# Modulation sums finished a quarter later, constants of the convolution loaded first, and the bias rows stored in three pieces

## The chip, the cores and the metric

The kernel runs on 1 core of one Trainium2 chip. The metric is the device time of one execution in microseconds (us). Before the change three runs took 3175.70, 3193.27 and 3194.81 us (median 3193.27); the execution that the profiler recorded took 3181.62 us.

## The reference, cut to what matters

One layer of a streaming trunk, on 2048 prompt tokens and 8 x 16 sample tokens, all in float32. What the change touches is the start (the modulation and the first normed tiles), the constants of the convolution, and the relative bias of the attention.

```python
def trunk_layer(x, c, conv_left, s0, band_cache, w_mod, b_mod, ..., conv_w, ..., rel_bias, w_out, w_up, w_down):
    sh1, sc1, g1, sh2, sc2, g2 = modulation(c, w_mod, b_mod)   # split(silu(c) @ w_mod + b_mod, 6)
    h = rmsnorm(x, norm1_g) * (1 + sc1) + sh1
    proj = h @ w_in
    o_a, conv_state, s = mixer_a(proj, conv_left, s0, conv_w, ...)   # conv of width 4, gated delta rule
    ...
    o_b = band_attention_prompt(qb, kb, vb, rel_bias)                # scores + bias on clipped distance
    x = x + g1 * (jnp.concatenate([o_a, o_b], axis=-1) @ w_out)
    h = rmsnorm(x, norm2_g) * (1 + sc2) + sh2
    x = x + g2 * (jnp.square(jax.nn.relu(h @ w_up)) @ w_down)

def rel_bias_matrix(rel_bias, qpos, kpos):
    d = jnp.clip(qpos[:, None] - kpos[None, :], -(CHUNK - 1), REL_MAX) + (CHUNK - 1)
    return rel_bias.astype(jnp.float32)[:, d]
```

## The kernel before

Tokens go in tiles of 128 rows: 16 prompt tiles and one sample tile (SMP). Phase 1 runs over six blocks of two or three tiles (the first block is tiles 0, 1 and SMP) and makes the projection with `w_in`, the convolution, the delta rule and the first attention; phase 2 runs over five blocks with `w_out`, `w_up` and `w_down`. Each matrix product is made of three matmuls on a high and a low part (`mm3`, L162 to L164, and L519 to L521 in the projection): the input's parts lie in `hT`, the weight's in `w`. `weights` (L166 on) loads a piece of some 0.5 MB into one of three `raw` buffers, ScalarE casts it to the high part (L175), GpSimd subtracts for the low part, and in the first block the low part is stored for later blocks (L184).

Before the first projection stands `modulation_start`: 16 pieces of `w_mod` (0.5 MB each, two halves `u` for each of four quarters `q` of scale and shift) are loaded through `mod_load` (L282), multiplied (`mps`, L288), added to `rows`, and `mod_finish` turns each finished quarter by a matmul (`ptm`, L317) into the columns of `modT`. In it stand also the loads of the three `x` tiles of block one (L261) and, at the end, the constants of the convolution (`conv_consts`: `cwt`, then transposes `psc` on TensorE, L455 and L456). Then `load_hT` norms each tile, transposes it (`psh`, L346), scales it with `modT` (`htmp`) and splits it into `hT`.

`rel_bias` (L1093 on) is called once, at the head of block two. It loads the 8 rows of the bias table (`ext`), makes 8 reversed and padded rows of 768 elements with two DVE copies (L1099, L1100), stores them to `s_ext` in DRAM (L1101), and reads them back shifted, DRAM to DRAM, as `s_bias` (8 x 128 x 640, L1102) and `s_bs` (L1103). The attention reads `s_bias` and `s_bs` from the end of phase 1 on.

The order in which each engine's instructions stand is not that of the code: the tile framework's scheduler places them by its own estimate of time, and each engine then executes its list strictly in that order. All DMAs of the text are issued from one queue, SyncE's (SP); an instruction in it that waits holds up all behind it. PSUM tiles of tag `g` (`mps`, `psg`, `psq`) share three buffers.

Of the kernel before, what the change touches and what calls it, by code (L numbers as in the profile page):

```python
# [19 lines left out]
SMP = 16  # L20
NB = 8
SL = 16
# [16 lines left out]
NPRE = 9  # L39
# [12 lines left out]
class Trunk:  # L52
# [168 lines left out]
    def modulation_start(self, first, tiles, p0):  # L221
# [8 lines left out]
        load = lambda n: self.mod_load(*first[n], p0.tile([P, D], F32, tag="raw0", name="raw0", bufs=NPRE))  # L230
        rvs, xs = [], []
        for n in range(min(NPRE, len(first))):
            rvs.append(load(n))
# [21 lines left out]
        order = list(dict.fromkeys(c[0] for c in first))  # L255
        for n, (sec, q, u) in enumerate(first):
            if n + NPRE < len(first):
                rvs.append(load(n + NPRE))
            if n % 4 == 3 and len(xs) < len(tiles):
                x = self.hp.tile([P, D], F32, tag="x", name="x", bufs=self.nx)  # L260
                nc.sync.dma_start(x, self.x_src(tiles[len(xs)]))  # L261
                xs.append(x)
# [69 lines left out]
    def load_hT(self, tiles, xs, sh, sc):  # L332

        for j, t in enumerate(tiles):
            xn = self.normed(xs[j] if xs else None, t)
            self.load_b(j, self.load_a(t, xn, sh, sc))
            self.fill_step()

    def load_a(self, t, xn, sh, sc):
        nc = self.nc  # L340
        tmps = []
        for q in range(2):
            ks = slice(4 * q, 4 * q + 4)
            ps = self.pa.tile([P, 512], F32, tag=self.patag, name="psh").rearrange("p (k t) -> p k t", t=P)
            for k in range(4):
                nc.tensor.transpose(ps[:, k], xn[:, (4 * q + k) * P:(4 * q + k + 1) * P], self.ident)  # L346
            tmp = self.hp.tile([P, 4, P], F32, tag="htmp", name="htmp", bufs=2)
            tmps.append(tmp)
            if t == SMP:
                f = lambda a: a.rearrange("p k (b s) -> p k b s", s=SL)  # L350
                self.tt(f(tmp), f(ps), bcast(self.modT[:, sc, ks, 1:], 3, SL), ALU.mult)
                self.tt(f(tmp), f(tmp), bcast(self.modT[:, sh, ks, 1:], 3, SL), ALU.add)
            else:
                for k in range(4):
                    a, b = self.modT[:, sc, 4 * q + k, 0:1], self.modT[:, sh, 4 * q + k, 0:1]
                    if k % 2:
                        self.act(tmp[:, k], ps[:, k], AF.Identity, scale=a, bias=b)
                    else:
                        self.ts(tmp[:, k], ps[:, k], a, ALU.mult, b, ALU.add)
        return tmps  # L360

    def load_b(self, j, tmps):
        cs = slice(j * P, (j + 1) * P)
        for q, tmp in enumerate(tmps):
            ks = slice(4 * q, 4 * q + 4)
            self.split(self.hT[:, ks, 0, cs], self.hT[:, ks, 1, cs], tmp)
# [73 lines left out]
    def conv_consts(self, p0):  # L440
        nc, c, i = self.nc, self.p1, self.i
# [5 lines left out]
        for g in range(3):  # L447
            gs = slice(g * 512, (g + 1) * 512)
            t = p0.tile([24, D], F32, tag="cwt", name="cwt", bufs=3)
            w4, h24 = t[0:4, 0:512], t[0:24, 512:1024]  # L450
            nc.sync.dma_start(w4, i["conv_w"][0][:, gs])
            nc.sync.dma_start(h24, i["state_conv"][0].rearrange("b w c -> (b w) c")[:, gs])
            ps = self.pa.tile([P, 512], F32, tag="pa", name="psc")
            for k in range(4):
                nc.tensor.transpose(ps[:, k * 4:(k + 1) * 4], w4[:, k * P:(k + 1) * P], self.ident[0:4, 0:4])  # L455
                nc.tensor.transpose(ps[:, 64 + k * 24:64 + (k + 1) * 24], h24[:, k * P:(k + 1) * P], self.ident[0:24, 0:24])  # L456
            self.ts(self.cw[:, 4 * g:4 * g + 4], ps[:, 0:16].rearrange("p (k r) -> p k r", r=4), 0.5, ALU.mult)
            nc.vector.tensor_copy(self.hists[:, 4 * g:4 * g + 4], ps[:, 64:160].rearrange("p (k r) -> p k r", r=24))
# [569 lines left out]
    def phase1(self):  # L1028
        nc, tc = self.nc, self.tc
        with ExitStack() as st:  # L1030
# [12 lines left out]
            with tc.tile_pool(name="p0", bufs=1, side="right") as p0:  # L1043
                xs = self.modulation_start([(sec, q, u) for q in range(4) for sec in (1, 0) for u in range(2)],
                                           BLOCKS1[0], p0)
# [11 lines left out]
            self.load_hT(B[0], xs, 0, 1)  # L1057
# [34 lines left out]
    def rel_bias(self):  # L1092

        nc = self.nc
        x = self.hp.tile([P, D], F32, tag="big", name="ext", bufs=2)
        ext, rev = x[0:BH, 0:REL], x[32:32 + BH, 0:EXT]
        nc.sync.dma_start(ext, self.i["rel_bias"][0])
        nc.vector.memset(rev[:, EXT - 64:], 0.0)
        nc.vector.tensor_copy(rev[:, EXT - 64 - REL:EXT - 64], ext[:, ::-1])  # L1099
        nc.vector.tensor_copy(rev[:, 0:EXT - 64 - REL], bcast(ext[:, REL - 1], 1, EXT - 64 - REL))  # L1100
        nc.sync.dma_start(self.s_ext, rev)  # L1101
        nc.sync.dma_start(self.s_bias, dram_ap(self.s_ext, P, [[EXT, BH], [-1, P], [1, 640]]))  # L1102
        nc.sync.dma_start(self.s_bs, dram_ap(self.s_ext, P, [[EXT, BH], [-1, SL], [1, 528]]))  # L1103
# [497 lines left out]
```

## Time and profile before

| | us |
|---|---|
| runs, lowest / median / highest | 3175.70 / 3193.27 / 3194.81 |
| profiled execution | 3181.62 |
| its span in the trace | 3179.9 |
| TensorE (PE) busy | 3046.9 |
| VectorE (DVE) busy | 1764.0 |
| ScalarE (ACT) busy | 1472.8 |
| GpSimd (POOL) busy | 644.5 |

All times in the rows are those of the one profiled execution, in us from the start of its span. "Busy" is the time in which an engine has an instruction in hand; PEclk is the clock that TensorE was granted, as a share of full speed. In a list of instructions a bracket gives the time that the engine sat idle before one and what released it.

### The profile page before, as it was taken

How to read it: one execution, taken by the hardware profiler on the slowest of the kernel's cores; microseconds unless marked ns; L12 is line 12 of the kernel's file. 1: busy time of each engine (PE TensorE's matmuls, PEld its weight loads, DVE VectorE, ACT ScalarE, POOL GpSimd, SP SyncE). 2: the span in 40 equal slices, each digit the busy share in tenths (PEclk: the TensorE clock that was granted, in tenths of full speed). 3: DMA queues.
4: the chain of work that ended last, by engine and by line, in shares of the span. 5: the costliest groups of instructions: out<-in, count | busy, mean ns of one | idle time of the engine just before them, and what ended most of it. 6: DMA issues, size and time to landing. Idle time of an engine off the chain costs nothing.

```text
span 3179.9 us, 52984 instructions
## 1 busy us (share of the span) xinstructions
PE 3046.9 (96%) x19649; PEld 2701.7 (85%) x19649; DVE 1764.0 (55%) x4222; ACT 1472.8 (46%) x2803; POOL 644.5 (20%) x517
## 2 busy tenths in 40 slices
PE   6999999999889989999999999999999999999998
PEld 4998989899889878888999888888988877888887
DVE  4775677667878663674356752454745433442223
ACT  3654545555466555545455353444354333333222
POOL 3631211121342247653222200000000000000000
PEclk9999999999999989999999999999999999999999
DMA  8798897888788778876777765666666676856654
GB/s 289 239 294 268 258 284 228 253 250 248 234 268 264 214 229 277 254 250 231 253 238 244 238 214 181 197 193 204 232 198 200 214 236 219 273 173 194 193 190 139
DMA packets 625947, 735.88 MB, mean 231 GB/s; under 512 B 59328, under 2 KB 483248, under 8 KB 623640
## 3 DMA queue, kind: packets, MB, share of 16 engines
q1 hardware_dynamic: 619928, 701.03, 70.1%
q0 software_dynamic: 5760, 31.46, 3.0%
q8 instruction: 155, 2.54, 0.3%
q14 instruction: 104, 0.85, 0.1%
HBM read 619.74 MB, written 115.52 MB: 231 GB/s over the span
## 4 chain that ended last, share of the span: by engine, by line
PE 70%; DMA 13%; DVE 9%; issue 3%; ACT 3%; POOL 1%; SPq 1%; POOLq 0%; ACTq 0%; DVEq 0%
PE psu L1483 7%; PE psu L1482 7%; PE psu L1484 7%; PE psd L164 7%; PE psd L162 7%; PE psd L163 7%; PE psb L163 2%; DMA raw<-in_w_up_dram 2%; PE psb L162 2%; PE psb L164 2%; PE pv L1286 2%; PE psS L1268 2%; PE psq L519 1%; PE psq L521 1%; PE psq L520 1%
## 5 line engine op out<-in xcount | busy, mean ns | idle before, releaser
L175 ACT CAST w<-raw 128x1024 fp32r<-128x1024 f32 (+1 forms) x528 | 552.1, 1047 | 387.1 <-PE psd L164 214.1
L1482 PE MATMUL psu<-hT,w 128*128 128x512 f32 (+2 forms) x1328 | 470.1, 356 | 1.9 <-ACT hT L104 1.7
L1484 PE MATMUL psu<-hT,w 128*128 128x512 f32 (+2 forms) x1328 | 468.5, 354 | 1.4 <-DMA w<-s_w_up 1.4
L1483 PE MATMUL psu<-hT,w 128*128 128x512 f32 (+2 forms) x1328 | 469.2, 354 | 0.4 <-DVE hT L82 0.3
L82 POOL TENSOR_TENSOR w<-raw,w 128x1024 fp32r<-128x1024 f32 (+1 forms) x162 | 391.6, 2427 | 351.3 <-ACT w L175 285.3
L162 PE MATMUL psd<-w,u 128*128 128x512 f32 x1088 | 430.9, 396 | 0.4 <-DVE y L82 0.3
L164 PE MATMUL psd<-w,u 128*128 128x512 f32 x1088 | 429.8, 396 | 0.0
L163 PE MATMUL psd<-w,u 128*128 128x512 f32 x1088 | 426.8, 392 | 2.1 <-POOL w L82 2.1
L79 DVE SCALAR_TENSOR_TENSOR psu<-psu,r 128x512 f32<-128x512 f32 (+2 forms) x160 | 98.9, 618 | 447.0 <-ACT r L92 446.9
L82 DVE TENSOR_TENSOR y<-y,psd 128x512 f32<-128x512 f32 x238 | 162.4, 685 | 260.3 <-PE psd L164 259.3
L1484 PEld LDWEIGHTS psu<-hT,w 128*128 128x128 f32 x1328 | 250.5, 189 | 33.2 <-DMA w<-s_w_up 1.7
L1482 PEld LDWEIGHTS psu<-hT,w 128*128 128x128 f32 x1328 | 250.1, 189 | 33.0 <-ACT hT L104 2.5
L1483 PEld LDWEIGHTS psu<-hT,w 128*128 128x128 f32 x1328 | 250.7, 189 | 31.9 <-issue 1.3
L92 ACT ACTIVATE r<-psu 128x512 f32<-128x512 f32 (+2 forms) x160 | 85.4, 534 | 375.7 <-issue 214.0
L163 PEld LDWEIGHTS psd<-w,u 128*128 128x128 f32 x1088 | 204.6, 188 | 47.8 <-POOL w L82 2.8
L164 PEld LDWEIGHTS psd<-w,u 128*128 128x128 f32 x1088 | 204.2, 188 | 46.4 <-issue 0.4
L162 PEld LDWEIGHTS psd<-w,u 128*128 128x128 f32 x1088 | 204.4, 188 | 43.8 <-DVE y L82 1.0
L162 PE MATMUL psb<-w,hT 128*128 128x256 f32 x816 | 236.0, 290 | 0.9 <-ACT hT L104 0.8
L163 PE MATMUL psb<-w,hT 128*128 128x256 f32 x816 | 234.7, 288 | 0.9 <-DMA w<-s_w_in 0.9
L164 PE MATMUL psb<-w,hT 128*128 128x256 f32 x816 | 233.4, 286 | 1.9 <-DVE hT L82 1.8
L519 PE MATMUL psq<-hT,w 128*128 128x384 f32 (+1 forms) x576 | 196.9, 342 | 8.1 <-ACT ba L499 8.1
L521 PE MATMUL psq<-hT,w 128*128 128x384 f32 (+1 forms) x576 | 193.6, 336 | 0.2 <-DMA w<-s_w_in 0.2
(315 smaller groups left out, 6459.5 us busy)
## 6 DMA issues: line engine op xcount, KB each, us to landing
raw<-in_w_up_dram SPq DMA_DIRECT2D x160, 512.0 KB
raw<-in_w_down_dram SPq DMA_DIRECT2D x160, 512.0 KB
raw<-in_w_in_dram SPq DMA_DIRECT2D x156, 512.0 KB
w<-s_w_down SPq DMA_DIRECT2D x128, 512.0 KB
w<-s_w_in SPq DMA_DIRECT2D x117, 512.0 KB
w<-s_w_up SPq DMA_DIRECT2D x96, 512.0 KB
raw<-in_w_out_dram SPq DMA_DIRECT2D x40, 512.0 KB
x<-in_x_prompt_dram SPq DMA_DIRECT2D x38, 512.0 KB
```

The source lines that it names most:

```text
L79: (eng or self.nc.vector).scalar_tensor_tensor(out, in0, scalar, in1, op0, op1)
L82: (eng or self.nc.vector).tensor_tensor(out, in0, in1, op)
L92: self.nc.scalar.activation(out, in_, func, **kw)
L162: mm(out, lh, rh, start=first, stop=False)
L163: mm(out, lh, rl, start=False, stop=False)
L164: mm(out, ll, rh, start=False, stop=last)
L175: nc.scalar.copy(w[:, 0, 0:n], r)
L519: mm(pc, wh, hT[:, k, 0, 0:T], start=(k == 0), stop=False)
L521: mm(pc, wl, hT[:, k, 0, 0:T], start=False, stop=(k == KT - 1))
L1482: mm(ps[:, c0:c1], wh, h2[:, k, 0, c0:c1], start=(k == 0), stop=False)
L1483: mm(ps[:, c0:c1], wh, h2[:, k, 1, c0:c1], start=False, stop=False)
L1484: mm(ps[:, c0:c1], wl, h2[:, k, 0, c0:c1], start=False, stop=(k == KT - 1))
```

## The change

1. In `modulation_start` the loads come in another order and from more buffers: the constants of the convolution (`cwt`, now two whole loads instead of six pieces) stand behind the second piece of `w_mod`; 12 pieces of `w_mod` are asked for at once (10 own buffers and two of tag `big`) instead of 9, the three `x` tiles in between, and the last four pieces follow as buffers come free.
2. `mod_finish` of a section is called one section later than its sum, so that the next matmuls stand ahead of it. As soon as scale and shift of two quarters are done, half of each `x` tile (4 of 8 pieces of 128 columns) is transposed, scaled and split; before, whole tiles came after all quarters. `conv_consts` is called in the middle, with 12 transposes of 28 rows instead of 24.
3. `rel_bias` is called three times, at the head of blocks two, three and four, with 3, 3 and 2 heads. Its rows lie in a buffer of tag `htmp` instead of `big`, the long row is written in two pieces: four small DVE instructions a call instead of three in all, and five DMAs a call instead of four in all.

```diff
-NPRE = 9
+NPRE = 10
...
+        def load(n):
+            pool, tag, bufs = (self.hp, "big", 2) if n in (NPRE, NPRE + 1) else (p0, "raw0", NPRE)
+            rvs.append(self.mod_load(*first[n], pool.tile([P, D], F32, tag=tag, name="raw0", bufs=bufs)))
+
+        for n in range(min(NPRE + 2, len(first))):
+            load(n)
+            if n % 4 == 3 and len(xs) < len(tiles):
+                x = self.hp.tile([P, D], F32, tag="x", name="x", bufs=self.nx)
+                nc.sync.dma_start(x, self.x_src(tiles[len(xs)]))
+                xs.append(x)
             if n == 1:
+                cwt = p0.tile([28, 1536], F32, name="cwt")
+                nc.sync.dma_start(cwt[0:24], i["state_conv"][0].rearrange("b w c -> (b w) c"))
+                nc.sync.dma_start(cwt[24:28], i["conv_w"][0])
...
+        xs = [self.normed(x, t) for x, t in zip(xs, tiles)]
+        done = []
+
+        def finish():
+            sec, q, row = done.pop(0)
+            self.mod_finish(sec, q, row, self.gp, "g")
+            if sec == first[-1][0] and q % 2:
+                for j, t in enumerate(tiles):
+                    self.load_bq(j, q // 2, self.load_aq(t, xs[j], 0, 1, q // 2))
...
             self.mod_mm(ps, rvs[n], u, u == 0, u == 1)
+            if n == 7:
+                self.conv_consts(cwt)
+            if n + NPRE + 2 < len(first):
+                load(n + NPRE + 2)
             if u:
                 row = rows[:, order.index(sec), q * 256:(q + 1) * 256]
                 self.tt(row, row, ps, ALU.add)
-                self.mod_finish(sec, q, row, self.gp, "g")
-        self.conv_consts(p0)
-        return xs
+                done.append((sec, q, row))
+                if len(done) > 1:
+                    finish()
+        finish()
...
-                if bi == 1:
-                    self.rel_bias()
+                if 1 <= bi <= 3:
+                    self.rel_bias(3 * bi - 3, min(3 * bi, BH))
...
+    def rel_bias(self, h0, h1):
+        nc = self.nc
+        m, k = h1 - h0, EXT - 64 - REL
+        x = self.hp.tile([P, 4, P], F32, tag="htmp", name="ext", bufs=2).rearrange("p a b -> p (a b)")
+        ext, lo, hi = x[0:m, 0:REL], x[32:32 + m], x[64:64 + m, 0:EXT - 512]
+        rev = ext[:, ::-1]
+        nc.sync.dma_start(ext, self.i["rel_bias"][0][h0:h1])
+        nc.vector.tensor_copy(lo[:, 0:k], bcast(ext[:, REL - 1], 1, k))
+        nc.vector.tensor_copy(lo[:, k:], rev[:, 0:512 - k])
+        nc.vector.tensor_copy(hi[:, 0:EXT - 576], rev[:, 512 - k:])
+        nc.vector.memset(hi[:, EXT - 576:], 0.0)
+        nc.sync.dma_start(self.s_ext[h0:h1, 0:512], lo)
+        nc.sync.dma_start(self.s_ext[h0:h1, 512:], hi)
+        o = h0 * EXT + P
+        nc.sync.dma_start(self.s_bias[h0:h1], dram_ap(self.s_ext, o, [[EXT, m], [-1, P], [1, 640]]))
+        nc.sync.dma_start(self.s_bs[h0:h1], dram_ap(self.s_ext, o, [[EXT, m], [-1, SL], [1, 528]]))
```

The scheduler's lists change with it. The first place is SP's queue at the start, from the last pieces of `w_mod` to the fourth piece of `w_in` (before the change; `ext` is the load of the bias table):

```order
L282 DMA raw_189<-in_w_mod_dram 128x4x256
L435 DMA alog<-in_a_log_dram 128x4
L282 DMA raw_196<-in_w_mod_dram 128x4x256
L436 DMA dtb<-in_dt_bias_dram 128x4
L174 DMA raw<-in_w_in_dram 128x4x264 x2
L174 DMA raw<-in_w_in_dram 128x8x128
L1097 DMA ext<-in_rel_bias_dram 8x320
L282 DMA raw_207<-in_w_mod_dram 128x4x256
L373 DMA x<-in_x_prompt_dram 128x1024
L184 DMA s_w_in<-w 128x1056
L174 DMA raw<-in_w_in_dram 128x8x128
```

The same place now:

```order
L302 DMA raw_210<-in_w_mod_dram 128x4x256
L302 DMA raw_218<-in_w_mod_dram 128x4x256
L302 DMA raw_224<-in_w_mod_dram 128x4x256
L443 DMA gdng<-in_gdn_norm_g_dram 128x1
L446 DMA qkg<-in_qn_g_dram 128x64
L447 DMA qkg<-in_kn_g_dram 128x64
L451 DMA alog<-in_a_log_dram 128x4
L452 DMA dtb<-in_dt_bias_dram 128x4
L174 DMA raw<-in_w_in_dram 128x4x264 x2
L174 DMA raw<-in_w_in_dram 128x8x128
L389 DMA x<-in_x_prompt_dram 128x1024 x2
L184 DMA s_w_in<-w 128x1056
```

All 16 pieces of `w_mod` now stand ahead of the small loads and of `w_in`, and the bias table is not in this stretch. The second place is SP's queue a little later, where the bias rows were stored (before):

```order
L174 DMA raw<-in_w_in_dram 128x8x128
L1102 DMA s_bias<-s_ext 1024x1x640
L1103 DMA s_bs<-s_ext 128x1x528
L297 DMA mrow<-in_b_mod_dram 9x256
L184 DMA s_w_in<-w 128x1024
L174 DMA raw<-in_w_in_dram 128x8x128
L373 DMA x<-in_x_prompt_dram 128x1024
```

and where the first of the three pieces stands now, in block two:

```order
L1115 DMA s_ext<-ext 3x512
L1116 DMA s_ext<-ext 3x256
L512 DMA s_sg<-sgw 128x256
L174 DMA raw<-in_w_in_dram 128x8x128
L179 DMA w<-s_w_in 128x1024
L174 DMA raw<-in_w_in_dram 128x8x128
L179 DMA w<-s_w_in 128x1024
L174 DMA raw<-in_w_in_dram 128x8x128
L1118 DMA s_bias<-s_ext 384x1x640
L1119 DMA s_bs<-s_ext 48x1x528
L678 DMA A<-s_U 32x4x32 x12
```

In the pieces for blocks three and four two rows and one row stand between the stores of `s_ext` and the copy to `s_bias`. The third place is DVE at the end of the modulation (before; `rows` are the sums, `bst` statistics of an `x` tile):

```order
L1099 COPY ext<-ext 8x320
L1100 COPY ext<-ext 8x384
L79 SCALAR_TENSOR_TENSOR modT<-ptm,rowT 128x18
L89 TENSOR_SCALAR htmp<-psh,modT 128x128
L82 TENSOR_TENSOR rows<-rows,mps 128x256
L378 BN_STATS bst<-x 128x6 x2
L82 TENSOR_TENSOR hT_98<-htmp,hT_98 128x4x128
L324 COPY modT<-ptm 128x18
```

and now:

```order
L79 SCALAR_TENSOR_TENSOR modT<-ptm,rowT 128x18
L87 TENSOR_SCALAR alog<-alog 128x4
L82 TENSOR_TENSOR htmp<-psh,modT 128x512
L82 TENSOR_TENSOR htmp<-htmp,modT 128x512
L89 TENSOR_SCALAR htmp<-psh,modT 128x128
L82 TENSOR_TENSOR rows<-rows,mps 128x256
L82 TENSOR_TENSOR hT_98<-htmp,hT_98 128x4x128
L344 COPY modT<-ptm 128x18
```

The two copies of `ext` no longer stand ahead of the last sum and of what turns it into `modT`; much of the scaling of the first half of the tiles stands ahead of it instead.

## Rows read from the trace of the kernel before

**Rows 1.** The page: busy time, DMA share in 40 slices, chain of waits.

```profile
PE 3046.9 (96%) x19649; PEld 2701.7 (85%) x19649; DVE 1764.0 (55%) x4222; ACT 1472.8 (46%) x2803; POOL 644.5 (20%) x517
...
DMA  8798897888788778876777765666666676856654
...
PE 70%; DMA 13%; DVE 9%; issue 3%; ACT 3%; POOL 1%; SPq 1%; POOLq 0%; ACTq 0%; DVEq 0%
```

**Rows 2.** Busy time in stretches of 10 us: PE, PEld, DVE, ACT, POOL, PEclk, DMA share, GB/s.

```profile
40.00:50.00 10.00, 4.24 (x23) 3.36 (x24) 8.81 (x13) 4.04 (x9) 5.88 (x4) 0.58 0.89 279
...
70.00:80.00 10.00, 1.90 (x8) 1.58 (x7) 4.29 (x12) 3.41 (x10) 2.35 (x1) 0.78 0.99 335
```

**Rows 3.** Chain that ended last, 28 to 90 us: start, duration, what.

```profile
33.54 7.19 DMA ext<-in_rel_bias_dram
40.76 2.60 DVE ext L1099
43.36 2.41 DVE ext L1100
...
62.39 13.29 DMA x<-in_x_prompt_dram
```

**Rows 4.** Instructions of PE in order of time, 0 to 90 us: start, duration.

```profile
42.08 1.08 PE L288 MATMUL mps<-raw,cT 128*32 128x256 f32 x8 [2.90 <-DMA raw<-in_w_mod_dram]
...
47.75 0.86 PE L317 MATMUL ptm<-sel,rows 128*128 128x9 f32 x4
48.46 0.57 PE L162 MATMUL psg<-w,hT 128*128 128x264 f32 x1
...
70.25 0.33 PE L521 MATMUL psq<-hT,w 128*128 128x384 f32 x1
78.68 0.69 PE L519 MATMUL psq<-hT,w 128*128 128x384 f32 x1 [8.10 <-ACT ba L499]
...
82.61 0.34 PE L519 MATMUL psq<-hT,w 128*128 128x384 f32 x1
...
84.54 0.34 PE L521 MATMUL psq<-hT,w 128*128 128x384 f32 x1
```

**Rows 5.** Instructions of SP's queue, 0 to 90 us: start, time to issue.

```profile
45.80 0.29 SPq L1101 DMA_DIRECT2D s_ext<-ext  x1
...
50.38 0.84 SPq L1102 DMA_DIRECT2D s_bias<-s_ext  x1
51.28 8.49 SPq L1103 DMA_DIRECT2D s_bs<-s_ext  x1
```

**Rows 6.** DMA from 0 to 45 us in 40 slices, and issues with their sizes.

```profile
GB/s 0 29 125 357 379 260 198 344 349 351 348 349 347 349 349 381 378 363 402 358 381 356 229 352 306 108 61 159 243 189 356 383 364 341 295 325 387 402 349 324
...
raw<-in_w_mod_dram SPq DMA_DIRECT2D x16, 512.0 KB
x<-in_x_prompt_dram SPq DMA_DIRECT2D x3, 512.0 KB
```

**Rows 7.** Instructions of ACT and of POOL in order of time, 0 to 90 us.

```profile
37.23 1.07 ACT L175 CAST w<-raw 128x1056 fp32r<-128x1056 f32 x1 [0.42 <-DMA raw<-in_w_in_dram]
...
38.38 7.19 POOL L82 TENSOR_TENSOR w<-raw,w 128x1056 fp32r<-128x1056 f32 x3 [8.95 <-ACT w L175]
```

**Rows 8.** Size of the copy to s_bias, from the list of DMA issues.

```profile
s_bias<-s_ext SPq DMA_DIRECT2D x1, 2560.0 KB
```

**Rows 9.** Busy time in stretches where the pieces now stand, columns as in rows 2.

```profile
230.00:240.00 10.00, 9.85 (x69) 8.81 (x68) 6.87 (x15) 6.10 (x16) 1.97 (x2) 1.00 0.77 225
...
250.00:260.00 10.00, 8.10 (x50) 7.07 (x48) 2.92 (x6) 5.16 (x11) 0.00 (x0) 0.66 1.02 278
...
400.00:410.00 10.00, 10.00 (x59) 10.00 (x58) 4.66 (x21) 1.62 (x3) 1.92 (x1) 1.00 1.09 324
...
490.00:500.00 10.00, 10.00 (x93) 9.72 (x92) 7.90 (x20) 5.85 (x17) 0.00 (x0) 1.00 0.67 191
```

**Rows 10.** Who waited for whom, PE, 225 to 265 us.

```profile
PE ptT L789 <- DMA A<-s_U: 0.2, 1, 0.2
```

More of the change, by code (lines that the diff above doesn't have):

```diff
@@ L255, in modulation_start @@
         order = list(dict.fromkeys(c[0] for c in first))
-        for n, (sec, q, u) in enumerate(first):
[L257 to L262, printed above, removed]
+        xs = [self.normed(x, t) for x, t in zip(xs, tiles)]
[6 more added lines that the diff above has]
+                    self.load_bq(j, q // 2, self.load_aq(t, xs[j], 0, 1, q // 2))
+        for n, (sec, q, u) in enumerate(first):
             if u == 0:
@@ L330, in x_src, with load_aq @@
         return self.i["x_prompt"][0, t * P:(t + 1) * P, :]
[L332 to L337, printed above, removed]
     def load_a(self, t, xn, sh, sc):
+        return [self.load_aq(t, xn, sh, sc, q) for q in range(2)]
+    def load_aq(self, t, xn, sh, sc, q):
         nc = self.nc
[L341 to L344, printed above, removed]
-            for k in range(4):
[L346 to L360, printed above, removed]
@@ new lines, in load_aq @@
+        ks = slice(4 * q, 4 * q + 4)
+        ps = self.pa.tile([P, 512], F32, tag=self.patag, name="psh").rearrange("p (k t) -> p k t", t=P)
+        for k in range(4):
+            nc.tensor.transpose(ps[:, k], xn[:, (4 * q + k) * P:(4 * q + k + 1) * P], self.ident)
+        tmp = self.hp.tile([P, 4, P], F32, tag="htmp", name="htmp", bufs=2)
+        if t == SMP:
+            f = lambda a: a.rearrange("p k (b s) -> p k b s", s=SL)
+            self.tt(f(tmp), f(ps), bcast(self.modT[:, sc, ks, 1:], 3, SL), ALU.mult)
+            self.tt(f(tmp), f(tmp), bcast(self.modT[:, sh, ks, 1:], 3, SL), ALU.add)
+        else:
+            for k in range(4):
+                a, b = self.modT[:, sc, 4 * q + k, 0:1], self.modT[:, sh, 4 * q + k, 0:1]
+                if k % 2:
+                    self.act(tmp[:, k], ps[:, k], AF.Identity, scale=a, bias=b)
+                else:
+                    self.ts(tmp[:, k], ps[:, k], a, ALU.mult, b, ALU.add)
@@ L362, in load_b, with load_bq @@
+        return tmp
     def load_b(self, j, tmps):
-        cs = slice(j * P, (j + 1) * P)
         for q, tmp in enumerate(tmps):
-            ks = slice(4 * q, 4 * q + 4)
-            self.split(self.hT[:, ks, 0, cs], self.hT[:, ks, 1, cs], tmp)
+            self.load_bq(j, q, tmp)
+    def load_bq(self, j, q, tmp):
+        cs, ks = slice(j * P, (j + 1) * P), slice(4 * q, 4 * q + 4)
+        self.split(self.hT[:, ks, 0, cs], self.hT[:, ks, 1, cs], tmp)
     def normed(self, x, t, st=None):
@@ L438, in phase1_consts, with conv_consts @@
         self.ts(self.alog, self.alog, -1.0, ALU.mult)
-    def conv_consts(self, p0):
-        nc, c, i = self.nc, self.p1, self.i
+    def conv_consts(self, t):
+        nc, c = self.nc, self.p1
         self.cw = c.tile([P, 12, 4], F32, name="cw")
@@ L446, in conv_consts @@
         self.hists = c.tile([P, 12, NB * 3], F32, name="hists")
[L447 to L452, printed above, removed]
-            ps = self.pa.tile([P, 512], F32, tag="pa", name="psc")
[L454 to L458, printed above, removed]
+        for g in range(6):
+            gs = slice(g * 256, (g + 1) * 256)
+            ps = self.pa.tile([P, 512], F32, tag="pa", name="psc")
+            for k in range(2):
+                nc.tensor.transpose(ps[:, k * 28:(k + 1) * 28], t[0:28, gs.start + k * P:gs.start + (k + 1) * P], self.ident[0:28, 0:28])
+            pv = ps[:, 0:56].rearrange("p (k r) -> p k r", r=28)
+            self.ts(self.cw[:, 2 * g:2 * g + 2], pv[:, :, 24:28], 0.5, ALU.mult)
+            nc.vector.tensor_copy(self.hists[:, 2 * g:2 * g + 2], pv[:, :, 0:24])
     def conv(self, y, pre, c, n, sub=None):
@@ L1043, in phase1 @@
             with tc.tile_pool(name="p0", bufs=1, side="right") as p0:
-                xs = self.modulation_start([(sec, q, u) for q in range(4) for sec in (1, 0) for u in range(2)],
-                                           BLOCKS1[0], p0)
+                self.modulation_start([(sec, q, u) for q in range(4) for sec in (1, 0) for u in range(2)],
+                                      BLOCKS1[0], p0)
             self.mod_todo = [(sec, q, u) for sec in (2, 3, 4, 5) for q in range(4) for u in range(2)]
@@ L1056, in phase1 @@
             last = len(B) - 1
-            self.load_hT(B[0], xs, 0, 1)
             for bi, tiles in enumerate(B):
@@ L1089, in phase1 @@
         self.ap2 = self.ctx.enter_context(tc.tile_pool(name="p2att", bufs=1, space=bass.MemoryType.PSUM, side="right"))
-    def rel_bias(self):
+    def rel_bias(self, h0, h1):
         nc = self.nc
[L1095 to L1103, printed above, removed]
+        m, k = h1 - h0, EXT - 64 - REL
[12 more added lines that the diff above has]
+        nc.sync.dma_start(self.s_bs[h0:h1], dram_ap(self.s_ext, o, [[EXT, m], [-1, SL], [1, 528]]))
     def softmax(self, ap, ps, bias, n):
```

3 lines of the change are left out of this document (removed).

## The prediction

> **What bounds the kernel now.** I read the page first: TensorE (PE) is busy for 3046.9 of 3179.9 us and holds 70% of the chain that ended last [rows 1]. So only some 133 us of idle PE time are to be had in all, and an edit pays only where PE stands or runs at a low clock. Next the stretches of 10 us, to find where that is at the start. From 40 to 50 us PE is busy for 4.24 us and is granted 0.58 of its clock, from 70 to 80 us for 1.90 us at 0.78 [rows 2]. The chain between 28 and 90 us names the two causes, and both are the bias table [rows 3]. First, a chain goes from the load of `ext` (33.54, 7.19 us) through the two DVE copies (2.60 and 2.41 us). PE meanwhile finished its last but one piece of `w_mod`, waited 2.90 us for the last one until 42.08, and reached `ptm` only at 47.75 and the projection (`psg`) at 48.46, since the last sum stood behind the copies on DVE [rows 4]. Second, 13.29 us pass from the issue of an `x` tile of block two at 62.39 to its landing [rows 3], and its statistics stand on DVE ahead of the last `sgw`; that `sgw` and `ba` keep the PSUM buffer which the third group of `psq` needs, and PE stands for 8.10 us until 78.68 [rows 4]. The reader is to see on SP's queue why that tile was late: `s_ext` is issued at 45.80, `s_bias` at 50.38, and the issue of `s_bs` takes 8.49 us, until 59.77, with `w` and `x` loads queued behind [rows 5].
>
> **What the earlier and denser loads bring.** All 16 pieces of `w_mod` and three `x` tiles, 19 loads of 512 KB (the sample tile is one of them, of the same size), are 10.0 MB. Full slices of the start move some 350 GB/s [rows 6]. The first three of the 40 slices (3.4 us) bring next to nothing; 10.0 MB at 350 GB/s are 28.5 us, the small constants about 1 us, so the last piece of `w_mod` should land near 33 us instead of 42.08. Before, three pieces of `w_in` and the small loads stood ahead of it, and eight slices (the 23rd to the 30th: 229, 352, 306, 108, 61, 159, 243, 189) fell short of 350 GB/s by what is worth 3.7 us [rows 6]. The `w_in` pieces now come behind, 1.5 us each: the first lands at 34.5 us, or at 38.2 if that short stretch, in which the small loads were issued, comes back. ScalarE's cast takes 1.07 us and GpSimd's subtraction 7.19/3 = 2.40 us [rows 7], so the first low part is ready at 38.0 to 41.7 us and one more follows each 2.4 us. PE can begin with the high part before that, but not run freely. I take an effective start 8 us earlier, about 40.5. Bounds: 4.4 us if the loads gain nothing and only the copies are gone (last `mps` at 42.08 and 1.08 long, so `ptm` near 43.3 instead of 47.75); 12 us if PE starts on the high part at 36.5.
>
> **What the missing stall brings.** The stall is 8.10 us, and after it PE runs slowly: 12 matmuls from 78.68 to 82.61 take 3.93 us, the 11 from 82.61 to 84.54 take 1.93, so 0.175 each, and 1.8 us are lost on the 12 [rows 4]. Together 9.9 us. I count them whole: the third `x` tile of block two is now asked for when its buffer comes free, not behind a standing queue. Bounds: 9.9, or 4 if the statistics of that tile, which still stand ahead of the last `sgw` on DVE, are late again by half.
>
> **What costs nothing.** TensorE's 12 fewer transposes and DVE's six more small constant copies lie in the first 35 us, in which PE waits for DMA anyway: the cover is the landing of `w_mod` at 33 us; without it they would be worth some 2 us. The two `cwt` loads move ahead of 14 pieces and delay them by less than 1 us, which I counted. Halved tiles and the later `mod_finish` move PE, DVE and ACT work under the same cover, and take a wait of PE for the sums off each quarter.
>
> **What the three pieces cost where they stand now.** The data are the same: 2560 KB of `s_bias` [rows 8] read and written, with `s_bs` 5.8 MB, at the 324 GB/s of a crowded stretch 18 us of DMA, which now fall in blocks two to four near 230, 400 and 490 us of the old trace (there stand the neighbours that the new order shows). Those stretches have DMA shares of 0.77, 1.09 and 0.67, and of 1.02 some 20 us behind the first [rows 9]. A piece of three heads needs 6.6 us. The full share is about 1.1, so the first piece finds about 3 us of room within 10 us, the second none, the third 4, and the rest pushes `w` pieces back. Against that stand four `w` buffers, and PE waited for DMA only 0.2 us between 225 and 265 us although DMA was as busy [rows 10]. SP itself also stands: from `s_ext` to `s_bias` 4.6 us passed before [rows 5]; in the second and third call two rows and one row lie between, so nearly all of it is a wait in the queue, and with it 3/8 of the 8.49 us, together up to 7.8 us in which no weight is asked for. One `psq` group is 24 matmuls of 0.175 us, 4.2 us a weight, so three weights in hand cover 12.6 us. Bounds: 0 (all hidden) and 18 (all DMA time exposed). I take 4, nearer to the 0.2 us of rows 10.
>
> On DVE the copies come back as nine in three calls. Before they took 2.60 and 2.41 us for 8 rows [rows 3], while GpSimd's three subtractions ran without a gap from 38.38 to 45.57 [rows 7]; where they go now GpSimd is busy for 1.97, 1.92 and 0.00 us of 10 [rows 9]. By the old durations a call costs DVE 7.5 us, and the same 12.6 us of PSUM and weights in hand cover it, so I count 0. The Trainium skill ("SBUF — State Buffer", section Who interferes with whom) says that a DVE copy in a two-port mode and a GpSimd instruction exclude each other for the whole instruction. The trace agrees so far: the copies end with the subtractions (45.77 and 45.57). By that rule the nine would be short here and the 0 is safe; by the old durations it rests on the cover. Against the split speaks another page ("DMA: Bandwidth & Descriptors", section Two DMAs through the same engine are not ordered): a DMA that reads what another wrote has to wait for its semaphore, so three calls pay three such waits. The trace shows one, the 4.6 us of rows 5; three would be 14 us of standing queue, which is the fourth case below.
>
> **The sum.** 3181.6 - 8 - 9.9 + 4 = 3167.7 us against the profiled execution. That one lies 11.7 us under the median of the runs shown, and 4.7 under the mean of the four times (3186.4). I forecast a median of new runs, so I add 4.7: 3172 us, 0.7% under the old median and 0.4% under the mean. The scheduler also moves rows all through phase 1; for that I count 0, and 6 us either way.
>
> **The rivals.**
> - The start gains, the moved bytes give it back: PE keeps standing for `w` in blocks two and three. For it: DMA share 1.09 near 400 us. Against: rows 10. All 18 us exposed: 3181.6 - 17.9 + 18 = 3182, with the 4.7 us 3186.
> - The change does not do what it says in its second half: `x` is late again and the stall only moves. For it: the order on DVE is the same at that place. Against: what kept SP is gone. 3181.6 - 8 + 4 = 3178, with 4.7 us 3182.
> - Everything comes off: 12 + 9.9 + 2 us and nothing given back: 3158, with 4.7 us 3162.
> - Slower: SP's queue stands in each call for `s_ext` and in `s_bs`, 7.8 us three times, 23 us, and the 18 us of bytes come on top: 3181.6 - 17.9 + 41 = 3205, with 4.7 us 3209. It decides once a standing queue outlasts the 12.6 us of weights in hand, so when DMA is full at the moment of the wait. Near 400 us it is; near 490 it is not.
>
> **How the numbers follow.** Forecast 0.62; bytes give it back 0.13; stall stays 0.09; everything comes off 0.12; slower 0.04. The range goes from 3152 (the best case less 10 us of run-to-run spread; the runs shown spread over 19 us) to 3195 (the first two rivals and the same spread); the slowest case lies outside. A measurement of this kernel can tell about 1% from no change, 32 us. Faster by over 1% is under 3161: most of the best case's lower half and a little of the forecast's, 0.10. Slower by over 1% is over 3225: 0.02. Within 1%: 0.88.
>
> **What would show it.** In the profile after, the last `mps` should begin near 33 us and the first `psg` between 36 and 41; no wait of PE above 3 us between there and 90 us; clock 1.0 from 70 to 80 us; SP's `s_bs` issues of about 3 us each. PE waits for `w` behind the new `s_bias` rows would show the second case, a wait of `psq` for `ba` or `sgw` the third. The prediction is wrong if the first 100 us gain under 8 us, or if PE's idle time between 200 and 550 us grows by over 10.

## The result and the profile after

The changed kernel takes 3222.51 us at the median (4 runs, 3215.62 to 3226.73), the kernel before 3190.07 us in the same comparison: a ratio of 1.0107 with a 95% interval of 1.0069 to 1.0145. It is slower by 32 us, where 3172 and a small gain were forecast, and it lies outside the range. The profiled execution took 3222.25 us, with a span of 3220.5 at a mean granted clock of 0.973.

To see where the time goes, I matched the instructions of PE in the two traces (same line, tiles and shape, n-th with n-th) and took the start after less the start before. The table gives medians over stretches of 50 us, named by their first microsecond in the trace of before; a negative number means that the row's kernel is ahead. The other rows are the experiments below. Each row rests on one execution: the one of before is 8.5 us quicker than that kernel's median (3181.62 against 3190.07), the one of e1_spread16 5 us slower than its own (3182.09 against 3177.09), so the last columns are not the differences of the medians.

```
lag behind before, us      50    150    200    250    350    400    500    550    900   1000   1200   1450   3050
after                    -8.8  -10.5   -9.2   -3.9   -2.3    6.4   16.6   21.6   28.8   36.4   41.0   45.9   40.5
e2_mod_only              -7.3    0.3    4.0   -0.9   -1.8   -4.8    1.9    1.9   -2.5   -0.1    1.0   -1.3   -3.0
e3_split_only            -1.3    1.1   -1.4    5.2    4.6   13.2   32.0   34.7   36.1   37.1   48.9   52.6   52.2
e1_spread16             -10.1  -11.8  -10.0   -8.4   -6.2   -3.1    0.3    1.6   -1.1    3.3    6.4    5.8    0.7
e6_spread4              -10.4  -11.9  -10.1   -1.6    0.9   10.5   13.5   14.8    6.8   13.7   16.2   14.9   14.0
e6_spread2               -9.8  -12.0   -9.5    6.4    8.9   26.8   32.4   36.5   27.6   31.3   33.1   30.7   28.1
e7_pool_queue            -9.0  -10.5   -8.7   -3.1    1.7    7.5   18.5   23.9   27.8   35.8   41.4   42.2   42.2
e9_two_calls             -9.0  -10.4   -8.9   -2.4    0.1    9.4   13.4   13.4   21.7   26.5   27.2   32.9   30.3
e10_split_spread         -1.8   -1.9   -3.8   -2.8   -0.8    2.2    6.0    7.0    6.2   19.1   24.6   29.8   26.5
```

So the start gains some 10 us and keeps it to 200 us. By 550 us another 31 are lost, from -9.2 to +21.6. In medians over 10 us three steps stand out where the three calls of `rel_bias` are: -9.4 to -3.9 near 240, -2.3 to 6.4 near 410 and 16.9 to 21.6 near 530, together 18.9 us. Another 10.5 us (6.4 to 16.9) go between 430 and 520, most of them before the changed kernel issues its third copy at 514.65. A second, slower loss of 24 us follows between 550 and 1450.

**The start.** PE's instructions in order of time (start, duration, what; in brackets its idle time and who ended it). They answer to [rows 4]:

```profile
34.58 1.08 PE L308 MATMUL mps<-raw,cT 128*32 128x256 f32 x8 [0.41 <-DMA raw<-in_w_mod_dram]
...
38.35 1.08 PE L308 MATMUL mps<-raw,cT 128*32 128x256 f32 x8
...
40.44 0.48 PE L162 MATMUL psg<-w,hT 128*128 128x264 f32 x2
...
52.56 0.39 PE L162 MATMUL psg<-w,hT 128*128 128x264 f32 x1 [1.94 <-ACT hT L104]
...
68.12 0.33 PE L533 MATMUL psq<-hT,w 128*128 128x384 f32 x1
73.00 0.55 PE L566 MATMUL ptq<-ident,kq 128*128 128x128 f32 x3 [4.54 <-DVE kq L79]
...
74.08 0.52 PE L531 MATMUL psq<-hT,w 128*128 128x384 f32 x1
74.40 0.52 PE L532 MATMUL psq<-hT,w 128*128 128x384 f32 x1
```

The projection begins at 40.44 us against 48.46, and the stall of 8.10 us for `ba` is gone. In its place PE stands 4.54 us for `kq`, and after it runs matmuls 0.32 us apart, against 0.175 before the stand. The granted clock there is 0.50 (columns as in [rows 2]), the lower of the two levels (1.2 GHz of 2.4):

```profile
75.00:77.00 2.00, 2.00 (x8) 2.00 (x8) 2.00 (x3) 0.39 (x1) 1.87 (x2) 0.50 0.66 224
```

DVE and POOL show what `kq` waited for:

```profile
60.87 2.25 DVE L79 SCALAR_TENSOR_TENSOR u<-x 128x12 f32<-128x12 f32 x1
...
64.69 2.19 DVE L82 TENSOR_TENSOR z<-u,z 128x12 f32<-128x12 f32 x1
...
67.32 2.49 DVE L79 SCALAR_TENSOR_TENSOR u<-u,w2s 128x12 f32<-128x12 f32 x2
...
69.99 0.16 DVE L79 SCALAR_TENSOR_TENSOR u<-u,w2s 128x12 f32<-128x12 f32 x1
...
72.39 0.55 DVE L79 SCALAR_TENSOR_TENSOR kq<-psq,y 128x384 f32<-128x384 f32 x1
```

```profile
60.69 2.40 POOL L82 TENSOR_TENSOR w<-raw,w 128x1024 fp32r<-128x1024 f32 x1 [3.33 <-ACT psq L538]
64.44 2.41 POOL L82 TENSOR_TENSOR w<-raw,w 128x1024 fp32r<-128x1024 f32 x1 [1.34 <-ACT w L175]
67.21 2.37 POOL L82 TENSOR_TENSOR w<-raw,w 128x1024 fp32r<-128x1024 f32 x1 [0.36 <-ACT w L175]
```

Three instructions of twelve elements a row, which elsewhere in this chain take 0.16 us, take over 2 us each; the first two end with the subtraction on GpSimd (63.12 and 63.09; 66.88 and 66.85). Before, GpSimd was busy for 8.28 us between 50 and 75 us, now for 15.88. The order on DVE matters as well: before, `z<-u,z` took 2.04 us beside a subtraction too, but `kq` stood ahead of it there and did not wait:

```profile
80.69 0.56 DVE L79 SCALAR_TENSOR_TENSOR kq<-psq,y 128x384 f32<-128x384 f32 x1
...
81.63 2.04 DVE L82 TENSOR_TENSOR z<-u,z 128x12 f32<-128x12 f32 x1
```

**The three steps.** SP's queue at the first call (start, time to issue), which answers to [rows 5]:

```profile
223.42 1.30 SPq L1118 DMA_DIRECT2D s_bias<-s_ext  x1
224.79 7.41 SPq L1119 DMA_DIRECT2D s_bs<-s_ext  x1
232.24 13.19 SPq L678 DMA_DIRECT2D A<-s_U  x12
```

The DMA from 225 to 250 us in 40 slices of 0.6 us, first the busy share in tenths of the 16 engines and then GB/s:

```profile
DMA  9999993212112113332323222112301212356679
GB/s 346 331 399 338 314 274 107 91 74 82 74 78 82 74 79 102 95 98 83 94 83 99 92 81 82 74 74 81 67 13 19 32 31 47 108 159 84 59 236 347
```

While SP has loads to issue, the DMA falls to some 75 to 105 GB/s and one to three tenths, for about 14 us. The trace's DMA records name the reason. The copy `s_bias<-s_ext` is made of rows of 2560 bytes, 0.103 us each, and they run in as many places at once as the copy has heads: 384 rows in 12.8 us at the first call (3.1 at once on the mean), 384 in 13.1 at the second (3.0), 256 in 13.25 at the third (2.0). Before, 1024 rows took 13.27 us, 7.9 at once. A piece of three heads thus lasts as long as the whole of eight, 128 rows one after the other. The trace of before had it to be read; this is its DMA from 50 to 75 us:

```profile
DMA  8999999997555555555799689955569789999789
GB/s 227 220 220 301 380 426 370 347 342 252 215 205 209 209 205 205 213 201 205 284 397 356 234 290 381 350 208 201 217 229 265 273 344 385 368 395 344 232 245 346
```

Nine slices stand at five tenths and 201 to 215 GB/s: half of the 16 engines' time is used, as with 8 of them at work. The waits of PE in the changed kernel around the three calls (us in total, times, longest), which answer to [rows 10]:

```profile
PE ptT L801 <- DMA A<-s_U: 8.8, 2, 8.5
...
PE psq L533 <- DMA w<-s_w_in: 10.1, 1, 10.1
...
PE kS L832 <- DVE E L82: 5.3, 1, 5.3
```

Each is one long stand, in 215 to 265, 380 to 460 and 490 to 560 us. Before, the longest in these three were 1.8 us, 2.9 us and none:

```profile
PE pw L796 <- ACT TW L92: 1.8, 1, 1.8
...
PE ptq L554 <- DVE kq L79: 2.9, 1, 2.9
```

The third stand is an indirect one. The chain behind `E` begins with a small load that took 8.09 us to land, at DMA shares of 1.02 to 1.07; the third copy had ended at 529.7:

```profile
534.17 8.09 DMA X<-s_vt
```

The stretches of 25 us show that the clock falls with the first two (columns as in [rows 2]):

```profile
225.00:250.00 25.00, 16.20 (x92) 14.23 (x91) 6.31 (x12) 6.16 (x17) 0.00 (x0) 0.80 0.43 127
...
395.00:420.00 25.00, 14.89 (x76) 14.52 (x76) 6.78 (x26) 6.17 (x14) 2.96 (x2) 0.80 0.65 197
```

Before, these stretches had PE busy for 24.85 and 22.08 us at clocks of 1.00 and 0.93, with DMA shares of 0.88 and 1.07:

```profile
225.00:250.00 25.00, 24.85 (x190) 22.05 (x189) 17.26 (x48) 12.36 (x31) 2.04 (x2) 1.00 0.88 247
...
395.00:420.00 25.00, 22.08 (x114) 20.50 (x113) 17.59 (x58) 9.82 (x24) 2.96 (x2) 0.93 1.07 322
```

The loss between the second and the third step is of another kind. PE stands for three short waits (0.6, 2.4 and 1.2 us) and then works for 15 us at a clock of 0.50, with no copy of bias rows under way:

```profile
490.00:505.00 15.00, 14.27 (x116) 11.97 (x117) 7.91 (x20) 8.52 (x19) 0.00 (x0) 0.50 0.65 191
```

### The profile page after: what moved, and what is told of

Its sections match the earlier page's. It is cut to its first block, busy times and chain, and to the rows that moved or that the text cites. A ratio compares the mean times of both kernels' runs of the same rounds, so it can differ in the third digit from the quotient of the medians.

```text
span 3220.5 us, 52996 instructions
## 1 busy us (share of the span) xinstructions
PE 3068.7 (95%) x19637; PEld 2719.4 (84%) x19637; DVE 1782.4 (55%) x4237; ACT 1472.6 (46%) x2803; POOL 646.0 (20%) x517
## 4 chain that ended last, share of the span: by engine, by line
PE 69%; DMA 13%; DVE 9%; ACT 3%; issue 2%; SPq 2%; POOL 2%; ACTq 0%; DVEq 0%; POOLq 0%
PE psu L1498 7%; PE psu L1500 7%; PE psu L1499 7%; PE psd L164 7%; PE psd L162 7%; PE psd L163 7%; DMA raw<-in_w_up_dram 2%; PE pv L1302 2%; PE psq L531 2%; PE psS L1284 2%; PE psq L532 2%; PE psq L533 1%; PE pso L162 1%; PE psb L162 1%; PE psb L163 1%
## 5 line engine op out<-in xcount | busy, mean ns | idle before, releaser
L533 PE MATMUL psq<-hT,w 128*128 128x384 f32 (+1 forms) x576 | 194.0, 337 | 10.1 <-DMA w<-s_w_in 10.1
```

Of the source, the lines that this page charges most:

```text
L533: mm(pc, wl, hT[:, k, 0, 0:T], start=False, stop=(k == KT - 1))
```

## The experiments

The theory (A in the expectations): this copy from DRAM to DRAM is spread over as many DMA engines as its outermost dimension has entries, here heads. Three short copies then hold two or three engines for 13 us each, and every load over all 16 that is queued later ends no sooner than its share on those. The rivals: the bytes themselves and the standing of SP's queue for `s_ext` (B); the new order of the work (C).

**e1_spread16: the changed kernel, each head's copy with an outermost dimension of 16.** The rows of `s_ext` are stored 16 times, so that the outermost dimension steps forward from one stored row to the next while the rows inside still step back.

```
-        nc.sync.dma_start(self.s_bias[h0:h1], dram_ap(self.s_ext, o, [[EXT, m], [-1, P], [1, 640]]))
+        for h in range(m):
+            nc.sync.dma_start(self.s_bias[h0 + h].rearrange("(a b) c -> a b c", a=16),
+                              dram_ap(self.s_ext, o + h * 16 * EXT, [[EXT - 8, 16], [-1, 8], [1, 640]]))
```

> The changed kernel with one thing altered: each row of s_ext is stored 16 times, so that each head's copy to s_bias has an outer dimension of 16 (and s_bs as well), one copy a head. Theory A (a copy runs on as many DMA engines as it has heads, each engine moves 128 rows of 0.103 us, 13 us however few the heads, and the transfers behind it in the queue end no sooner): the copies of a call take 2 to 3 us together instead of 12.8 to 13.3, PE's waits of 8.5 us for A and of 10.1 us for w are gone, and the 25 to 30 us lost near the three calls come back: 1.000 to 1.006 of the kernel before. Theory B (the queue stands for s_ext and the bytes are too many for these blocks): the waits for s_ext and the bytes are the same and there are more issues, so 1.009 to 1.013. Theory C (the new order of phase 1 costs it, wherever the copies are): 1.008 to 1.012, with the losses at the same places.

Measured: 3177.09 against 3187.19 us, 0.9966 [0.9951, 0.9981], faster than both kernels, and better than theory A had it; B and C, which forecast a loss of 0.8 to 1.3%, miss. The three copies take 3.4, 3.9 and 4.2 us (2 to 3 were expected), and the DMA stays nearly full at the second call, where it had fallen to 75 GB/s:

```profile
DMA  8983989998999799999999999999999999999999
```

(395 to 420 us). The step near 240 us shrinks from 5.3 to 1.6 us, that at 400 from 8.7 to 3.1; a wait of 5.7 us for `w` stays there. The order of the work on every engine is again another one than the changed kernel's, so this run alone does not part the copies from the order; the runs with 2 and 4 below do.

**e2_mod_only and e3_split_only: each half of the change alone.** The first leaves `rel_bias` in one call at its old place, the second leaves the start as before.

```
e2:  the diff without   -  if bi == 1: self.rel_bias()   and the new rel_bias
e3:  only               +  if 1 <= bi <= 3: self.rel_bias(3 * bi - 3, min(3 * bi, BH))   and the new rel_bias
```

> Parts 1 and 2 alone: the changed kernel with the bias rows made and stored in one call at the head of block two, as before. Theory A: one copy of 13 us on 8 DMA engines instead of three on 3, 3 and 2, so no loss near 230, 400 and 500 us: 0.994 to 1.000 of the kernel before. Theory B: the same, 0.994 to 1.000. Theory C: the order of phase 1 is new here too, 1.002 to 1.010.

> Part 3 alone: the kernel before with the three calls of 3, 3 and 2 heads. Theories A and B: some 10 us gained at the start, where the copy is gone, and 30 to 45 us lost from the three calls on: 1.005 to 1.012 of the kernel before. Theory C: 0.997 to 1.003.

Measured: the start alone 3183.28 us, 0.9987 [0.9969, 1.0004], no difference that can be told; the split alone 3232.57 us, 1.0151 [1.0119, 1.0183], more than any theory expected. The loss belongs to the split. The start's own gain needs the bias table out of its way: alone it is 7.3 us ahead at 50 us and level at 150. And moving the table away gains nothing alone either (+1.1 at 150): the two gains don't add up from the halves, they come together.

**e4_before_spread16: the kernel before, its one call spread over 16.**

```
-        nc.sync.dma_start(self.s_ext, rev)
+        nc.sync.dma_start(self.s_ext, bcast(rev, 1, 16))
```

and the copy by heads as in e1.

> The kernel before, one call, with each head's copy spread over 16 engines as in e1_spread16. Theory A: the copy that held 8 engines for 13.3 us now takes some 7 us on all 16; a stall of 8 us at 70 to 78 us gets shorter: 0.996 to 1.000 of the kernel before. Theories B and C: no change, 0.998 to 1.002.

Measured: 3187.97 us, 1.0005 [0.9988, 1.0021]. The hoped for gain is not there. The copies still take 13.4 us (61.12 to 74.53), in two bursts of 6.2 and 4.9 us, though the DMA's busy share is now seven to nine tenths meanwhile, not five (50 to 75 us, slices of 0.6 us):

```profile
DMA  4799544679999999778999998999999999999999
```

Other loads share the engines. So at that place the spread bought no time that can be told.

**e6_spread2 and e6_spread4: e1 with 2 or 4 in place of 16.** Every engine runs the same instructions in the same order as in e1; only the shape of the copy differs.

```
-            ... rearrange("(a b) c -> a b c", a=16),  [[EXT - 8, 16], [-1, 8], [1, 640]]
+            ... rearrange("(a b) c -> a b c", a=2),   [[EXT - 64, 2], [-1, 64], [1, 640]]
```

> e1_spread16 with one number altered: each head's copy to s_bias has an outer dimension of 2 instead of 16, so that it runs on 2 DMA engines; every engine's list of instructions is that of e1_spread16, row for row. Theory A (few engines make a copy long, and what is queued behind it ends no sooner): three heads take 3 x 64 rows x 0.103 us = 19.8 us, two heads 13.2, so the loss is at least that of the changed kernel: 1.008 to 1.018 of the kernel before. Theory B (the wait for s_ext, the bytes and the issues cost it): all as in e1_spread16, 0.995 to 0.999. Theory C (the order costs it): the order is that of e1_spread16, 0.995 to 0.999.

> The same with an outer dimension of 4. Theory A: 9.9 us for three heads and 6.6 for two, of which the weights in hand cover a part: between e1_spread16 and e6_spread2, 0.998 to 1.006 of the kernel before. Theories B and C: 0.995 to 0.999.

Measured: 3214.23 us with 2, 1.0078 [1.0053, 1.0102]; 3191.21 with 4, 0.9999 [0.9982, 1.0015]; 3177.09 with 16. Against the runs of before made beside each, that is +25, +2 and -10 us: the same bytes in the same order cost 12 us more on 4 and 35 us more on 2. The steps at the three calls, read as for the changed kernel, are 2.0, 3.1 and 3.1 us with 16 (8 together), 8.9, 9.6 and 3.2 with 4 (22) and 16.2, 17.9 and 9.3 with 2 (43). The copies take 19.2, 19.8 and 13.2 us on 2 and 10.0, 11.1 and 7.2 on 4. Three heads at 64 rows of 0.103 us, two abreast, are 19.8 us one head after the other, and the records show 2.0 rows at once: so the three copies of a call seem to use the same two engines, not two each. The waits for weights near 400 us, in e1, with 4 and with 2:

```profile
PE psq L533 <- DMA w<-s_w_in: 5.7, 1, 5.7
```

```profile
PE psq L533 <- DMA w<-s_w_in: 12.3, 1, 12.3
```

```profile
PE psq L533 <- DMA w<-s_w_in: 20.6, 1, 20.6
```

These runs also bound what the copies explain. With 4 the steps at the calls (22 us) are no smaller than the changed kernel's (18.9), yet that kernel ends level with before. And with 2 the copies are longer than the changed kernel's, yet the ratio is no higher (1.0078 [1.0053, 1.0102] against 1.0107 [1.0069, 1.0145]). So a part of the changed kernel's loss is not in the steps that the copies make.

**e7_pool_queue: the changed kernel with the two copies issued from GpSimd's queue.**

```
-        nc.sync.dma_start(self.s_bias[h0:h1], ...)
+        nc.gpsimd.dma_start(self.s_bias[h0:h1], ...)
```

> The changed kernel with the copies to s_bias and s_bs issued from GpSimd's queue instead of SP's; heads, sizes and calls are as in the changed kernel. Theory A in its first form (later transfers of SP's own queue stand behind the long copy, and SP stands in the issue of s_bs): the other queue lets them pass, 0.996 to 1.003 of the kernel before. Theory A in its second form (the two or three DMA engines themselves are taken for 13 us, whatever the queue): 1.005 to 1.011. GpSimd's own wait for s_ext should cost little, it is busy for under 2 of 10 us there.

Measured: 3222.30 us, 1.0112 [1.0080, 1.0143], as slow as the changed kernel. SP no longer stands in `s_bs`, yet PE's wait for `A<-s_U` is the same 8.8 us in total, now with a longest of 5.8:

```profile
PE ptT L801 <- DMA A<-s_U: 8.8, 2, 5.8
```

SP's queue shows that the stand has only moved to the next loads:

```profile
222.15 1.16 SPq L174 DMA_DIRECT2D raw<-in_w_in_dram  x1
223.36 17.87 SPq L678 DMA_DIRECT2D A<-s_U  x12
```

7.41 + 13.19 = 20.6 us in the changed kernel, 17.87 here. On this queue the first copy is of 192 packets of 5120 bytes, 2.8 at once, 13.4 us: no shorter; the other two take 16.8 and 17.1 us. The other queue gained nothing.

**e9_two_calls: the changed kernel with calls of 4 and 4 heads.**

```
-                if 1 <= bi <= 3:
-                    self.rel_bias(3 * bi - 3, min(3 * bi, BH))
+                if 1 <= bi <= 2:
+                    self.rel_bias(4 * bi - 4, 4 * bi)
```

> The changed kernel with two calls of four heads (blocks two and three) in place of calls of 3, 3 and 2 heads. Theory 'few engines a copy': each piece has 4 heads, so 4 engines for the same 13 us (128 rows of about 0.103 us), two such stretches in place of three: the copies take 12.5 to 14 us each on about 4.0 engines, the lag of the third stretch (+15 us in the changed kernel between 475 and 550) is not there, and the ratio is 1.001 to 1.008, under the 1.011 of three calls. Rival 'by bytes': the same 5.8 MB are moved, so the loss is that of three calls, 1.009 to 1.014, and a piece of 4 heads lasts a third longer than one of 3.

Measured: 3207.41 us, 1.0059 [1.0037, 1.0082]. The copies take 13.2 and 13.3 us at 4.0 at once: a third more bytes in each, no more time. There is no third step (9.4 at 400, 13.4 at 500 and at 550 us); of the 15 us that the changed kernel loses between 400 and 550, only 4.7 were a step at its third call. The ratio is in the theory's range and its interval under the rival's: the rival by bytes falls.

**e5_one_call_spread: e1 with one call of eight heads in block two.**

```
-                if 1 <= bi <= 3:
-                    self.rel_bias(3 * bi - 3, min(3 * bi, BH))
+                if bi == 1:
+                    self.rel_bias(0, BH)
```

> e1_spread16 with one call of 8 heads at the head of block two instead of three calls; eight copies on 16 engines, about 7 us together, where the first of the three pieces stands. Theory A: no worse than e1_spread16, 0.994 to 0.999 of the kernel before; if the bytes in a crowded block cost something after all, 0.998 to 1.002.

Measured: 3193.89 us, 1.0011 [0.9996, 1.0027], slower than e1 by medians, although its profiled execution is ahead of before until 1100 us (-5.3 at 1000) and of e1's from 350 to 1450. That execution loses 11 us between 1000 and 1200, and why, the trace does not tell; it is also 10 us quicker than the median of this kernel (3183.91 against 3193.89), so it cannot show all of the difference. What holds is that one call is not better than three once the copies are spread.

**e10_split_spread: the split alone (e3) with the copies spread as in e1.**

```
 e3, and in rel_bias:
+        for h in range(m):
+            nc.sync.dma_start(self.s_bias[h0 + h].rearrange("(a b) c -> a b c", a=16), ...)
```

> Part 3 alone (three calls in blocks two to four, the start as before), with every row of s_ext stored 16 times and one copy a head with an outer dimension of 16, as in the kernel that beat both. Part 3 alone with 3, 3 and 2 engines stood at 1.0151 [1.0119, 1.0183]. Theory 'few engines a copy': the loss was the engines' number, so it goes: each head's copy takes 3 to 5 us, no lag against before grows by more than 4 us over 225-260, 395-430 or 510-545, and the ratio is 0.997 to 1.004. Rival 'moving the work out of the start costs in itself' (the order of the work in blocks two to four, the DVE's copies, the wait for s_ext): the ratio stays over 1.008 although the copies are short. Both expect 0 to 5 us at the start from fewer bytes there.

Measured: 3210.31 us, 1.0066 [1.0044, 1.0088], between what the two theories expected. Up to 900 us the theory holds: copies of 3.3, 5.3 and 3.6 us, and the lag at 550 us is 7.0 against 34.7. But then 24 us are lost again, between 900 and 1450 us, long after the last copy. That is as much as the changed kernel loses between 550 and 1450, and short copies don't cure it. Against e1, which also has short copies and differs by the start, and with it in the order of all that follows, e10 is 32 us slower by medians (+22 and -10 against before). Three stretches of 50 us with their granted clock, 0.81, 0.91 and 0.80:

```profile
900.00:950.00 50.00, 45.43 (x395) 40.27 (x395) 30.04 (x89) 30.28 (x67) 15.52 (x17) 0.81 0.93 287
...
950.00:1000.00 50.00, 46.63 (x359) 44.32 (x358) 39.95 (x125) 30.14 (x71) 14.41 (x17) 0.91 0.54 170
...
1150.00:1200.00 50.00, 38.17 (x243) 34.30 (x242) 36.38 (x87) 27.21 (x54) 21.70 (x15) 0.80 0.62 199
```

Before, it was 0.90, 1.00 and 0.93 there; in the changed kernel 0.94, 0.79 and 0.77. No one wait of PE accounts for it.

## Why the prediction was wrong, point by point

**The loads at the start: right, but not all of it lasted.** An effective start 8 us earlier, about 40.5, was taken; `psg` began at 40.44, and the lag is -8.4 at 56 us. The last wait for a piece of `w_mod` ended at 34.58, near the 33 that was worked out; the last `mps` itself began at 38.35, behind transposes. From 64 to 70 us, just ahead of the old stall, the lag is -6.3: PE had stood 1.94 us for `hT` until 52.56 and then run some matmuls 0.32 us apart.

**The missing stall: half right, and mis-sized.** The wait for `ba` is gone, and DVE read the `x` tiles without a wait. Of the 9.9 us only about 4 came (-6.3 just ahead of the old stall, -10.4 from 120 us on). The prediction said that the stall goes and asked only whether the same tile would be late; it did not ask what stands next. That was the DVE chain from `ba` to `kq`, 12.3 us (60.66 to 72.94), three links of which sat behind GpSimd's denser subtractions, and on DVE `kq` now stood behind them. The Trainium skill ("SBUF — State Buffer", section Who interferes with whom) says that a DVE instruction with two SBUF inputs contends with a GpSimd instruction that reads SBUF; the trace agrees for `z<-u,z` (2.19 us, with a subtraction over it). The prediction used that section for the copies alone, and there its 0 was right: they took 0.35, 0.21 and 0.25 us.

**The three pieces: wrong, the step that failed.** The prediction priced them by bytes: 5.8 MB at 324 GB/s, 18 us between "all hidden" and "all exposed", and took 4; "a piece of three heads needs 6.6 us". It measured 12.8 to 13.3 us a piece whatever its heads, and steps of 18.9 us at the three calls. The bound of 18 was none, since it assumed that all engines work on the copy: with 2 abreast the same bytes make steps of 43 us. A row's time and the number of copies abreast were both in the trace of before (128 rows of 0.103 us behind each other, half of the engines busy), and cutting 8 heads into 3, 3 and 2 keeps the first and lowers the second. The runs show it by dose: 16, 4 and 2 abreast in one and the same order give -10, +2 and +25 us against before, and calls of 4 and 4 heads last as long as calls of 3.

The Trainium skill ("DMA: Bandwidth & Descriptors", sections Why a DMA increments its semaphore by 16 and not by 1 and Rules for kernel authors) has the rule: the slowest dimension that is not 1 sets how many engines a transfer uses, at most 16, and an outermost dimension of fewer confines it to at most that many. The trace agrees (8 heads 7.9, 4 heads 4.0, 3 heads 3.1, 2 heads 2.0). By it the sum would have held three stretches of 13 us on a few engines in place of 18 us of DMA spread over all. The prediction looked at that page for the wait between two transfers and not for this.

**The new order: put at nothing, and it was not.** "The scheduler also moves rows all through phase 1; for that I count 0, and 6 us either way." In the changed kernel 10.5 us are lost between the second and the third step, with PE at a clock of 0.50 for 15 us and no copy under way, and 24 us after 550. e6_spread4, with the same steps at the calls, has neither in that size (1.2 and 0.1 us), and e10 and e1, both with short copies, end 32 us apart. So something that comes with the new order, the clock included, seems to be worth more than 6 us; that it is the order itself is not shown.

**SP's queue.** The slower rival named the place, `s_bs` standing three times with weights queued behind, and came near (3209, against 3222.5), but at a chance of 0.04 and by another road: it let SP stand for `s_ext` and added the bytes. The stand in `s_bs` was put at 3/8 of 8.49 us, about 3; it was 7.41, 5.92 and 5.25 us, longer than the bytes explain; what it waits for is not shown. As e7 shows, the stand is a symptom: without it the same 8.8 us of PE's wait remain.

**The cover.** 12.6 us of weights in hand were to hide such a wait. Near 400 us PE still stood 10.1 us for `w`: after 13 us of copy the loads behind it came late too, and the stand in `A<-s_U` near 240 us is not covered by weights at all, since PE takes its work in order. The prediction's own mark, idle time of PE between 200 and 550 us growing by over 10, is met: 8.6 us before, 31.4 now, of which the three stands are 8.8, 10.1 and 5.3.

**What stays open.** That the loads which PE waits for queue behind the copy on the very same engines is inferred: the waits grow as the engines get fewer, and three copies in a row run two rows at once. No run puts a copy on engines of its own. And the 10.5 us ahead of the third step and the 24 us between 550 and 1450 us, more than the steps at the calls, are not settled. The 24 us don't follow the size of the earlier lag (e6_spread2 is 27.6 us behind at 900 and 30.7 at 1450, e10 goes from 6.2 to 29.8) nor the length of the copies. The instruction order differs between these kernels all through phase 1, and the clock is lower in some stretches; which is cause and which is effect was not tried. A run would tell that has the order of one kernel and the copies of another; only the e1 and e6 kernels share an order, and there the second loss is small whatever the copies (7 us in e1 between 900 and 1450, 8 with 4 abreast, 3 with 2).

## What to carry to other kernels

Before a transfer is cut, look at its outermost dimension and at the DMA's busy share while it runs: a flat stretch at five tenths was the sign here that 8 heads ran abreast, and cutting along that dimension made every piece as long as the whole. Give each piece an outermost dimension of 16, and then move it: with that a loss of 1.1% became a gain of 0.3%, though the order of the work changed too, and the split alone stayed 0.7% slower even so. A changed order of the work is a term of its own, and nothing here supports putting it at 0. When a stall is taken away, ask for the next link on the same path, here a DVE chain that shares time with GpSimd, and count only the gap between the two.

## What the runs showed of the hardware that was not expected

A copy of 384 rows and one of 1024 took the same 13 us (12.8 and 13.27), and the one of 256 rows 13.25. Three copies issued back to back with two abreast ran one after the other, 19.2 us for three, though most of the DMA stood idle (49 to 53 GB/s, one tenth):

```profile
DMA  9999999992111111111111111155212222111111
GB/s 397 332 315 323 353 389 329 306 228 66 49 53 53 49 53 53 49 49 57 49 49 53 53 49 53 53 117 150 77 51 74 76 72 69 60 49 53 53 49 49
```

(e6_spread2, 225 to 250 us; slices of 0.6 us.) Issued from GpSimd's queue instead of SP's, the copies took 13.4, 16.8 and 17.1 us.
